# A decoder trunk on one core: the order of twelve-matmul blocks in TensorE's queue

## The chip, the cores and the metric

The kernel runs on one NeuronCore of a Trainium2 chip. The metric is the time of one execution on the device in microseconds, the median of several. The engines are named as the profile names them: PE (TensorE; PEld is its weight load), DVE (VectorE), ACT (ScalarE), POOL (GpSimd) and SP (the queue that issues DMAs).

## What is computed

One inference step of a one-layer hybrid decoder trunk, for 1024 prompt positions and 8 decode positions, together T = 1032 columns, with 1024 features, in float32. Cut to what matters:

```python
def mixer(xn):                                   # xn = rmsnorm(x)
    qkv, z, xbc, dt = split(xn @ w_in)           # 1024 -> 7184 columns
    for g, (window, dil) in enumerate(((128, 1), (512, 4), (2048, 16))):
        q, k = rope(qkv[g, 0]), rope(qkv[g, 1])  # 8 heads of 64
        o[g], lse[g] = dilated_window_attention(q, k, qkv[g, 2])
    attn = merge(o, softmax(lse over g))
    y = ssd(silu(conv4(xbc)), dt)                # 16 heads, chunks of 128
    ssm = rmsnorm((y + d_skip * xs) * silu(z))
    return concat(attn, ssm) @ w_out             # 1536 -> 1024
x = x + rmsnorm(mixer(rmsnorm(x)))
x = x + rmsnorm((silu(h @ w_gate) * (h @ w_up)) @ w_down)   # h = rmsnorm(x), hidden 2816
```

The decode positions take part in the same products, attend to key and value caches and step an SSD state; the caches are also copied to the outputs, shifted by one row.

## The kernel before

Activations lie transposed, features on the 128 partitions and the T columns along the free axis, in three chunks of CW = 344 columns. Each large operand is split into a high part and a remainder (`wh` and `wl` of a weight, `hs` and `ls` of an activation; `xh`, `xl`, `hh`, `hl` and so on in the profile), and a product is the sum of three: high by high, remainder of the weight by high, high by remainder of the activation. `unit` (line 160) computes one 128 x 344 block of a product into a PSUM tile that way: for each of n blocks of 128 input features three matmuls, all at line 168. n is 8 for the products out of 1024 features, so 24 matmuls; 6 or 4 in the last product of the SwiGLU (18 or 12 matmuls), and 4 in the attention half of the output projection (12). `gemm` (line 181) loads one 128-column weight block (`load_w`, line 136), and for each chunk runs a unit in one of two PSUM tiles (`psg`) and copies or adds the result out.

The stages, in order of time: the norm of the input and the first 12 column blocks of `w_in` (`xb`, convolution of SSD); then, `pattern` (line 682) for the three attention patterns: for each of 4 head pairs (`hp`) `do_v`, `do_qk` for q and `do_qk` for k (three gemms of three units, copied to a row tile `rw` at line 576, of which there are two buffers), and `attend` (line 620). Beside the first pattern run the 16 calls of `ssd` (line 467), beside the others the decode scores. Then the 8 gemms for z, beside them the merge of the three patterns (written to `ah` and `al`, lines 848 and 849) and the decode attention over the cached values (line 869); then the output projection with its norm, and the SwiGLU in groups of hidden blocks, `pg` and `pu` for gate and up and `g` for the last product.

Work that is not a unit is called side work here. On PE it is many small matmuls and transposes: for `ssd`, `xt` (line 487), `gb` (493, 494), `yp` (513), `yo` (521) and `stp` (529); for attention, `sps` (636, scores of two tiles of 128 queries for each of two heads of 64 features), `ptp` (657, transposes of the exponentials), `nps` (670, by the values, 64 output rows per head), and `vtp` (594, transposes of the values, copied to `vt` at line 596). A tile of 128 queries (`j`, eight per head pair) goes sps, maximum (DVE, 642), exponential (ACT, 650), `ptp`, copy (661 or 663), `nps`. PSUM holds two `sps` tiles and one each for `ptp` and `nps`; q, k and v of two head pairs fit in SBUF. Rope of q and k is side work on ACT, POOL and DVE, and ends at line 610 with `qr`.

The order on every engine is laid out when the program is built. Each instruction carries a number, `tc.cur_priority`, and the framework walks along a timeline of its own model (`schedule_with_timeline_sim=True`): at each step an engine takes, of the instructions whose inputs and buffers are ready there, the one with the lowest number. On the chip each engine then runs its list in that fixed order and waits where an input is not there yet. The numbers come from counters that `prio` (line 54) takes up and puts back, so that within one kind the order is that of the program:

```python
ctr = {"evac": 1_000_000, "w": 5_000_000, "side": 10_000_000, "late": 20_000_000, "main": 50_000_000}
```

"evac" are the copies out of PSUM and the statistics of the norms (matmuls at lines 215, 921 and 990), "w" the loads and splits of weights, "side" the side work, "late" the merge and decode attention, and "main" the matmuls of `unit`, of line 361 (the dt columns) and of line 945 (the first units of the output projection, written out). So a unit's matmuls fill PE wherever no side instruction is ready.

Of the kernel before, what the change touches and what calls it, by code (L numbers as in the profile page):

```python
# [16 lines left out]
P = 128  # L17
# [19 lines left out]
RATE = (0.35, 0.52)  # L37
NEG = -1e30
SCALE = 0.125

PC_NORM = 0
PC_CW = PC_NORM + 5 * 8
# [5 lines left out]

def trunk(tc, a, o):
    nc = tc.nc  # L50
    ctr = {"evac": 1_000_000, "w": 5_000_000, "side": 10_000_000, "late": 20_000_000, "main": 50_000_000}

    @contextmanager
    def prio(kind):
        old, tc.cur_priority = tc.cur_priority, ctr[kind]
        yield
        ctr[kind], tc.cur_priority = tc.cur_priority, old
# [35 lines left out]
    for g in range(NG):  # L93
        w = WIN[g]
        n = (w - 1) * 1024
# [64 lines left out]
    def unit(ps, w, hs, ls, c, ch=CH):  # L160
        wh, wl = w
        c0, c1 = ch[c]
        n = len(hs)
        with prio("main"):
            for k in range(n):
                ws = slice(k * P, (k + 1) * P)
                for j, (x, y) in enumerate(((wh, hs[k]), (wl, hs[k]), (wh, ls[k]))):
                    nc.tensor.matmul(ps, x[:, ws], y[:, c0:c1], start=(k == 0 and j == 0),  # L168
                                     stop=(k == n - 1 and j == 2))

    gpools = [psg]
    ngp = [0]
# [1 line left out]
    def gps(name="g", cw=CW):  # L174
        q = gpools[ngp[0] % len(gpools)]
        ngp[0] += 1
        if q is psg:
            return q.tile([P, 512], F32, tag="g", name=name)[:, :cw]
        return q.tile([P, 512], F32, tag="ap", name=name)[:, :cw]

    def gemm(src, cols, hs, ls, evac, cc=(0, 1, 2), share=False):
        w = load_w(src, cols, share)
        for c in cc:
            ps = gps()
            unit(ps, w, hs, ls, c)
            with prio("evac"):
                next_copy(evac(c, ps))
# [110 lines left out]
    for m in range(12):  # L298
# [8 lines left out]
        if m == 0:  # L307
            gpools.extend((psg, psa, psa, pst, psn))
            begun = {}
            for c in range(3):  # L310
                for q in range(2):
                    begun[q, c] = gps()
                    unit(begun[q, c], first[q], xh, xl, c)
# [43 lines left out]
    for c, (c0, c1) in enumerate(CH):  # L357
        ps = gps("dps")
# [261 lines left out]
    def attend(g, hp, qr, kr, vt):  # L620
        nh = nhp.tile([P, S], F32, tag="nh", name="nh")
        for j in range(8):
# [16 lines left out]
            for h in range(2):  # L639
# [5 lines left out]
            i2 = slice(hp * 2, hp * 2 + 2)  # L645
            nc.vector.tensor_scalar(out=ngm[:, g, j, i2], in0=mx[:, g, j, i2], scalar1=-SCALE, scalar2=0.0,  # L646
                                    op0=ALU.mult, op1=ALU.add)
            for h in range(2):
                i = hp * 2 + h
                nc.scalar.activation(out=sm[:, h, :nk], in_=sm[:, h, :nk], func=AF.Exp, scale=SCALE,  # L650
                                     bias=ngm[:, g, j, i:i + 1], accum_out=den[:, g, j, i:i + 1])
# [105 lines left out]
    with prio("side"):  # L757
# [3 lines left out]
        for h in range(2):  # L761
            nc.vector.tensor_reduce(out=dmx[:, h:h + 1], in_=sal[:, h].rearrange("p g x -> p (g x)"), op=ALU.max,
                                    axis=AX.X)
        nc.vector.tensor_scalar(out=dmx, in0=dmx, scalar1=-SCALE, scalar2=0.0, op0=ALU.mult, op1=ALU.add)
        for h in range(2):
            sv = sal[:, h].rearrange("p g x -> p (g x)")
            nc.scalar.activation(out=sv, in_=sv, func=AF.Exp, scale=SCALE, bias=dmx[:, h:h + 1],
                                 accum_out=dde[:, h:h + 1])
# [5 lines left out]
        for g in range(NG):  # L774
# [3 lines left out]
                             start=True, stop=True)  # L778
# [26 lines left out]
    with prio("late"):  # L805
# [11 lines left out]
        for g in range(NG):  # L817
            t = cap.tile([P, 8, 8], F32, name=f"wg{g}")
            nc.vector.tensor_tensor(out=t, in0=sn[g][:, :, 0:8], in1=mm, op=ALU.subtract)
            nc.scalar.activation(out=t, in_=t, func=AF.Exp, scale=SCALE)  # L820
            wg.append(t)
# [113 lines left out]
    def ssm_w(m, share=False):  # L935
        return load_w(a["w_out"][m][:, 512:1536], 1024, share)

    ws = [ssm_w(m) for m in range(2)]
    pq = [[gps() for c in range(2)] for m in range(2)]
    with prio("main"):  # L940
        for k in range(KT):
            for m in range(2):
                for j in range(3):
                    for c in range(2):
                        nc.tensor.matmul(pq[m][c], ws[m][j == 1][:, k * P:(k + 1) * P],
                                         (sl if j == 2 else sh)[k][:, CH[c][0]:CH[c][1]],
                                         start=(k == 0 and j == 0), stop=(k == KT - 1 and j == 2))
# [45 lines left out]
    for c, (c0, c1) in enumerate(CH):  # L993
# [4 lines left out]
        for m in range(KT):  # L998

            def ev(c, ps, m=m, acc=acc):  # L1000
                r = nc.vector.tensor_tensor(out=mix[m][:, c0:c1], in0=mix[m][:, c0:c1], in1=ps, op=ALU.add)
                stat(mix[m][:, c0:c1], m == 0, acc, nc.vector)
                return r

            if m % 2 == 0:
                pair = kept[m] if m in kept else load_pair(m, False)
            ps = gps()
            unit(ps, [x[:, (m % 2) * 512:(m % 2 + 1) * 512] for x in pair], ahs, als, c)
            with prio("evac"):
                ev(c, ps)  # L1010
        with prio("evac"):
# [3 lines left out]
            for m in range(KT):  # L1015
                if m % 2 == 0:
                    x = np_.tile([P, 2, CW], F32, tag="xr", name="xr")
# [247 lines left out]
```

## Time and profile before

| | |
|---|---|
| median of 3 runs | 1928.76 us (1927.81 to 1932.84) |
| the profiled execution | 1929.59 us |
| its span, first to last instruction | 1927.8 us |
| instructions on PE | 11727 matmul records, 95% of the span busy |
| DVE, ACT, POOL busy | 53%, 38%, 20% |
| mean granted clock of PE | 0.979 |

The profile is of one execution. The busy time of PE is the union of its matmuls' records; consecutive matmuls overlap in it (a record of 0.32 us every 0.16 us), so a start-to-start distance tells more than a duration. A small float32 matmul or transpose stands as two records. "Idle before" is time in which the engine stood still before an instruction, with what released it. The granted clock is PE's clock as a share of 2.4 GHz.

### The profile page before, as it was taken

The page shows a single profiled execution, that of the slowest core. Times are in us where ns is not written, and L with a number is a line of the kernel's source. Part 1 is how long each engine was busy: PE and PEld are TensorE (multiplying, and loading weights), DVE is VectorE, ACT ScalarE, POOL GpSimd, SP SyncE. Part 2 cuts the span into 40 slices and gives each one's busy share as a digit, 9 for nine tenths or more (in the row PEclk, how much of TensorE's full clock was granted, in tenths as well). Part 3 has the DMA queues.
Part 4 walks back from the last instruction along what each step waited for, and adds up shares of the span by engine and source line. Part 5 has one row for each costly group of instructions (what it writes and reads, how often), then busy time and mean ns, then how long its engine had stood idle before and what let it go on. Part 6 is the DMA issues. An engine that isn't in the chain of part 4 may idle for free. (4 is left out here: it accounts for less than half of the span.)

```text
span 1927.8 us, 29260 instructions
## 1 busy us (share of the span) xinstructions
PE 1825.0 (95%) x11727; PEld 1709.3 (89%) x11727; DVE 1014.0 (53%) x1896; ACT 739.2 (38%) x1388; POOL 394.5 (20%) x277
## 2 busy tenths in 40 slices
PE   8999989999999899998879989999999999999994
PEld 6999878888888798887679989999999999999993
DVE  6544676757764544455774896331333333333348
ACT  5543554545554455665242353222221112211242
POOL 0000244543232311133533342000000000000025
PEclk9999999999999999999889999999999999999997
DMA  4322333443334433464754454347433643366362
GB/s 162 122 95 86 119 108 112 137 128 107 104 115 136 156 100 110 142 237 137 178 154 133 147 168 132 109 150 249 133 115 130 240 164 131 105 202 207 115 247 88
DMA packets 125544, 275.26 MB, mean 143 GB/s; under 512 B 17616, under 2 KB 83632, under 8 KB 124000
## 3 DMA queue, kind: packets, MB, share of 16 engines
q1 hardware_dynamic: 125408, 273.39, 43.4%
q8 instruction: 92, 1.51, 0.3%
q14 instruction: 44, 0.36, 0.1%
HBM read 235.86 MB, written 125.47 MB: 187 GB/s over the span
## 5 line engine op out<-in xcount | busy, mean ns | idle before, releaser
L168 PE MATMUL g<-xh,wh 128*128 128x344 f32 x1344 | 443.7, 330 | 9.7 <-ACT zt L893 5.5
L168 PE MATMUL g<-xl,wh 128*128 128x344 f32 x1344 | 440.4, 328 | 1.5 <-DVE xl L222 1.5
L168 PE MATMUL g<-xh,wl 128*128 128x344 f32 x1344 | 439.0, 327 | 0.5 <-DVE wl L157 0.5
L168 PEld LDWEIGHTS g<-xh,wh 128*128 128x128 f32 x1344 | 255.8, 190 | 19.3 <-ACT zt L893 6.1
L168 PEld LDWEIGHTS g<-xh,wl 128*128 128x128 f32 x1344 | 256.2, 191 | 11.3 <-issue 9.9
L168 PEld LDWEIGHTS g<-xl,wh 128*128 128x128 f32 x1344 | 256.3, 191 | 10.4 <-issue 7.4
L157 DVE TENSOR_TENSOR wl<-wr,wh 128x1024 fp32r<-128x1024 f32 (+1 forms) x133 | 163.0, 1226 | 124.9 <-ACT wh L156 124.7
L156 ACT CAST wh<-wr 128x1024 fp32r<-128x1024 f32 (+1 forms) x133 | 134.4, 1011 | 214.5 <-PE g L168 128.8
L168 PE MATMUL pg<-fh,wl 128*128 128x344 f32 x504 | 161.8, 321 | 0.2 <-DVE wl L157 0.2
L168 PE MATMUL pg<-fl,wh 128*128 128x344 f32 x504 | 161.8, 321 | 0.0
L168 PE MATMUL pu<-fl,wh 128*128 128x344 f32 x504 | 161.6, 321 | 0.0
L168 PE MATMUL pu<-fh,wh 128*128 128x344 f32 x504 | 161.2, 320 | 0.0
L168 PE MATMUL pu<-fh,wl 128*128 128x344 f32 x504 | 160.8, 319 | 0.0
L168 PE MATMUL pg<-fh,wh 128*128 128x344 f32 x504 | 158.5, 322 | 0.0
L1110 POOL TENSOR_TENSOR ow<-wr,ow 128x512 fp32r<-128x512 f32 x8 | 11.1, 1407 | 674.9 <-ACT ow L1109 674.9
L168 PE MATMUL g<-hl,wh 128*128 128x344 f32 x432 | 138.0, 319 | 0.0
L168 PE MATMUL g<-hh,wl 128*128 128x344 f32 x432 | 137.6, 319 | 0.0
L168 PE MATMUL g<-hh,wh 128*128 128x344 f32 x432 | 137.3, 320 | 0.0
L230 DVE TENSOR_TENSOR u<-pu,rf 128x344 f32<-128x344 f32 x66 | 34.1, 516 | 195.5 <-PE pu L168 195.5
L650 ACT ACTIVATE sm<-sm,ngm 128x128 f32<-128x128 f32 (+1 forms) x192 | 84.9, 443 | 108.3 <-DVE ngm L646 106.2
L606 POOL TENSOR_TENSOR sw<-sw,sin 128x1032 f32<-128x1032 f32 x24 | 74.9, 3122 | 247.6 <-ACT sw L605 184.1
L1079 ACT CAST hh<-s 128x344 fp32r<-128x344 f32 x66 | 31.7, 480 | 199.4 <-DVE s L1078 197.3
(323 smaller groups left out, 3710.7 us busy)
## 6 DMA issues: line engine op xcount, KB each, us to landing
out_skv<-in_cache SPq DMA_DIRECT2D x64, 1023.5 KB, 5.3
wr<-in_w_in SPq DMA_DIRECT2D x56, 512.0 KB, 3.8
wr<-in_w_fin SPq DMA_DIRECT2D x44, 512.0 KB, 3.8
out_skv<-in_cache SPq DMA_DIRECT2D x16, 1022.0 KB, 5.5
wr<-in_w_out SPq DMA_DIRECT2D x24, 512.0 KB, 4.1
wr<-in_w_fout SPq DMA_DIRECT2D x24, 384.0 KB, 4.2
e<-cs_d SPq DMA_DIRECT2D x16, 512.0 KB, 3.9
n_d<-nh SPq DMA_DIRECT2D x12, 512.0 KB, 4.2
```

What stands on the lines that cost most here:

```text
L156: nc.scalar.copy(wh[:, :cols], wr[:, :cols])
L157: nc.vector.tensor_tensor(out=wl[:, :cols], in0=wr[:, :cols], in1=wh[:, :cols], op=ALU.subtract)
L168: nc.tensor.matmul(ps, x[:, ws], y[:, c0:c1], start=(k == 0 and j == 0), stop=(k == n - 1 and j == 2))
L230: return nc.vector.tensor_tensor(out=dst, in0=ps, in1=r[:dst.shape[0], c0:c1], op=ALU.mult)
L606: nc.gpsimd.tensor_tensor(out=sw[:, 0:T], in0=sw[:, 0:T], in1=sin, op=ALU.mult)
L650: nc.scalar.activation(out=sm[:, h, :nk], in_=sm[:, h, :nk], func=AF.Exp, scale=SCALE, bias=ngm[:, g, j, i:i + 1], accum_out=den[:, g, j, ...
L1079: nc.scalar.copy(hh[:, c0:c1], s)
L1110: nc.gpsimd.tensor_tensor(out=wl, in0=src, in1=wh, op=ALU.subtract)
```

## The change

The twelve consecutive matmuls of a unit that begin at a multiple of twelve are kept together: the first keeps the number kind "main", the other eleven get the new kind "run", whose numbers lie behind "evac" and ahead of "w", "side" and "late". A unit of 24 is two such blocks, one of 12 is one, one of 18 a block of twelve and one of six. `unit` also returns its last matmul, which nothing uses. Lines 361 and 945 are as before.

```diff
@@ -37,6 +37,7 @@
 SCALE = 0.125
+RUN = 12
@@ -48,7 +49,7 @@
-    ctr = {"evac": 1_000_000, "w": 5_000_000, "side": 10_000_000, "late": 20_000_000, "main": 50_000_000}
+    ctr = {"evac": 1_000_000, "run": 3_000_000, "w": 5_000_000, "side": 10_000_000, "late": 20_000_000, "main": 50_000_000}
@@ -161,12 +162,14 @@
         n = len(hs)
-        with prio("main"):
-            for k in range(n):
-                ws = slice(k * P, (k + 1) * P)
-                for j, (x, y) in enumerate(((wh, hs[k]), (wl, hs[k]), (wh, ls[k]))):
-                    nc.tensor.matmul(ps, x[:, ws], y[:, c0:c1], start=(k == 0 and j == 0),
-                                     stop=(k == n - 1 and j == 2))
+        for k in range(n):
+            ws = slice(k * P, (k + 1) * P)
+            for j, (x, y) in enumerate(((wh, hs[k]), (wl, hs[k]), (wh, ls[k]))):
+
+                with prio("main" if (3 * k + j) % RUN == 0 else "run"):
+                    last = nc.tensor.matmul(ps, x[:, ws], y[:, c0:c1], start=(k == 0 and j == 0),
+                                            stop=(k == n - 1 and j == 2))
+        return last
```

## Rows read from the trace of the kernel before

**Rows 1.** The page, part 1: busy time, share and instructions of each engine.

```profile
PE 1825.0 (95%) x11727; PEld 1709.3 (89%) x11727; DVE 1014.0 (53%) x1896; ACT 739.2 (38%) x1388; POOL 394.5 (20%) x277
```

**Rows 2.** By stage: length, PE PEld DVE ACT POOL busy, granted clock, DMA, GB/s.

```profile
200.00:600.00 400.00, 383.21 (x2701) 329.18 (x2699) 269.06 (x629) 208.69 (x426) 162.86 (x112) 0.99 0.40 122
600.00:975.00 375.00, 346.60 (x2233) 304.42 (x2234) 199.92 (x455) 188.95 (x400) 107.54 (x58) 0.96 0.47 147
...
1177.00:1890.00 713.00, 709.85 (x4489) 709.38 (x4488) 251.11 (x399) 155.25 (x254) 21.17 (x16) 1.00 0.47 160
```

**Rows 3.** The same view for line 168 alone, the stage of side work.

```profile
200.90:970.90 770.00, 532.50 (x3003) 479.05 (x3002) 0.98 0.43 135
```

**Rows 4.** The chain that ended last, 1190 to 1205 us: start, us, what.

```profile
1193.35 3.78 PE pg L168 x24
```

**Rows 5.** Timeline of PE around two bursts: start, us, instruction [idle before].

```profile
453.18 0.32 PE L168 MATMUL g<-xh,wl 128*128 128x344 f32 x1
453.44 0.66 PE L670 MATMUL nps<-pt,vt 128*64 128x128 f32 x8
...
455.07 0.32 PE L168 MATMUL g<-xl,wh 128*128 128x344 f32 x1
455.22 0.60 PE L487 MATMUL xt<-ident,xg 128*128 128x128 f32 x4
...
456.01 0.41 PE L168 MATMUL g<-xh,wh 128*128 128x344 f32 x1
456.25 0.32 PE L168 MATMUL g<-xh,wl 128*128 128x344 f32 x1
```

**Rows 6.** Timeline of PE: the first and the last of 190 bursts.

```profile
200.95 0.66 PE L427 MATMUL dtp<-ident,dex 8*128 8x8 f32 x8
...
969.99 0.85 PE L921 MATMUL ptp<-acc,ones 128*128 128x344 f32 x2 [2.45 <-POOL acc L908]
```

**Rows 7.** Waits of PE, 200 to 975 us: total us, times, longest us.

```profile
PE sps L636 <- DVE qr L610: 9.9, 5, 3.8
PE xt L487 <- DMA xg<-xs_d: 7.4, 4, 2.3
PE nps L869 <- DVE cvt L868: 6.3, 3, 3.2
...
PE nps L670 <- DVE pt L663: 3.7, 3, 1.7
...
```

**Rows 8.** Windows (columns of rows 2), then timeline of PE at three places.

```profile
444.00:450.00 6.00, 6.00 (x59) 4.26 (x58) 4.42 (x4) 1.71 (x6) 5.18 (x2) 1.00 0.24 92
...
599.80:606.60 6.80, 5.13 (x20) 4.48 (x21) 5.66 (x14) 0.00 (x0) 3.28 (x2) 0.50 0.59 195
...
601.47 0.80 PE L636 MATMUL sps<-qr 64*128 64x128 f32 x4 [3.79 <-DVE qr L610]
...
444.11 0.66 PE L670 MATMUL nps<-pt,vt 128*64 128x128 f32 x8
...
449.84 0.42 PE L168 MATMUL g<-xh,wl 128*128 128x344 f32 x1
```

**Rows 9.** `ptp` by line, 756 to 800 us, and timeline of PE between two.

```profile
L657 PE MATMUL ptp<-ident,sm x16: 272/273/332, 760.3 to 791.8; 128*128 128x128 f32 x16
...
764.56 0.44 PE L657 MATMUL ptp<-ident,sm 128*128 128x128 f32 x2
...
769.18 0.44 PE L657 MATMUL ptp<-ident,sm 128*128 128x128 f32 x2
```

**Rows 10.** Timeline of ACT, second head pair.

```profile
287.89 0.61 ACT L596 COPY vt<-vtp 128x512 f32<-128x512 f32 x1
...
301.73 0.43 ACT L576 COPY rw<-g 128x344 f32<-128x344 f32 x1
```

**Rows 11.** Timeline of DVE and of PE where the merged attention is used.

```profile
1035.43 0.43 DVE L849 TENSOR_TENSOR al<-nt,ah 128x256 fp32r<-128x256 f32 x1
...
1049.88 0.32 PE L168 MATMUL g<-ah,wah 128*128 128x344 f32 x1
```

## The prediction

> **What bounds the kernel now.** I read the page first: TensorE (PE) is busy for 95% of the span, the next engine for 53% [rows 1]. So the time is PE's work plus the places where PE waits or works slowly. The table by stage says where those are [rows 2]: from 1177 us to 1890 us, the SwiGLU, PE shows no gap (709.85 of 713 us), and a unit of 24 long matmuls (line 168) takes 3.78 us there [rows 4], so one costs 0.157 us in a dense row. Nothing but long products stands in that stage, so keeping twelve together changes nothing in it, nor in most of the first 163 us. The change can act between about 200 and 970 us, where attention, SSD and decode (side work) share PE with 3003 long matmuls [rows 3].
>
> In that stage the timeline of PE shows 190 bursts of side instructions between long matmuls, the first at 200.95 us and the last at 969.99 us [rows 6]. Counted there, 74 of the 189 rows of long matmuls between two bursts have at most 12 of them, 88 have 13 to 24, and 27 have more. Three losses hang on the bursts:
> - A change-over. After a burst of transposes the next two long matmuls start 0.24 us apart (456.01 and 456.25) in place of 0.157: 0.08 lost. Eight `nps` matmuls start 0.26 us after the long one ahead of them (453.18 and 453.44): 0.10 lost on the way in [rows 5].
> - Waits in PE's fixed order: PE reaches a side instruction before its input is there. `sps` 9.9 us, `xt` 7.4, `nps` of decode 6.3, `nps` of attention 3.7: 27.3 us in 15 waits, the longest 3.8 [rows 7].
> - The clock. Granted 0.99 over 400 us and 0.96 over 375 us [rows 2] are together some 38 us at the lower of the two levels (1.2 GHz). In 599.8 to 606.6 us it is 0.50 all through, and PE stood still for 3.79 us of that, waiting for `qr`, up to 601.47 us [rows 8]: the clock falls where PE stands still.
>
> **The change part by part.** No instruction, DMA or wait is added or taken out, and SP, POOL, ACT and DVE keep their rules; only PE's order moves. The first of each twelve keeps the number of "main", behind all side work; the other eleven get 3 million, ahead of "w", "side" and "late" and behind "evac". So the 3003 long matmuls become 250 blocks of 12 x 0.157 = 1.88 us, and a side instruction that becomes ready inside a block waits for its end, 0.94 us on average. The statistics of the norms (L215, L921, L990) go at "evac" and still break in; the products at L361 and L945 are written apart and keep "main".
>
> *Fewer bursts.* Bursts that become ready in one block join. If 190 fall on 250 block ends at random, 250 x (1 - e^(-190/250)) = 133 ends carry one: 57 fewer at most. Steps of one chain can't join, since the second needs the first, so the other end is none fewer. I take 45, nearer the upper end because attention, SSD and decode are three chains side by side. A joined burst saves one way out and, for tiled operands, one way in: 0.08 to 0.20 us, say 0.15 [rows 5]. Gain 45 x 0.15 = 7 us; ends 0 and 11.
> The rows show that a burst that begins with 64-wide operands (`nps`) costs 0.10 us on entry, and one that begins with full 128 x 128 transposes starts 0.15 us after the last long matmul, so nothing [rows 5]. The Trainium skill, TensorEngine Tiling, section Key Properties, says that changing the tiling mode drains TensorE, which this agrees with. By that rule joined bursts still pay for each change between tiled and full operands inside them, so only the way out would be saved: 45 x 0.09 = 4 us in place of 7.
>
> *Waits in PE's order.* A side instruction that is placed up to 1.88 us later finds its input more often ready. A wait of x under 1.88 us shrinks on average to x^2/3.76, a longer one by 0.94 us. Their mean is 27.3 / 15 = 1.8 us (the four of `xt` come to 7.4 us with 2.3 the longest), so about half is left: 27 to some 14, gain 13 us. Ends: 0 (every input moves back as far as its reader) and 27.
>
> *The clock.* The 38 us at 1.2 GHz cost at most half of themselves, 19 us [rows 2], less where PE stands still anyway, as in 5.13 busy of 6.80 us [rows 8]. Where waits shrink, some of these stretches go: I take a quarter, 5 us; ends 0 and 10.
>
> *What gets later.* Each PE step of a side chain now waits for a block. Attention is the longest chain: transpose a tile's scores (`ptp`), copy, multiply (`nps`), next tile. In the last pattern eight `ptp` bursts (16 records) stand between 760.3 and 791.8 us, 4.5 us apart [rows 9], with 22 long matmuls between the two at 764.56 and 769.18 us [rows 9]. Rounded up to two blocks that is 24, 0.3 us more per tile and 2.4 us per head pair, 29 us over the 12 pairs. If the input is ready just after the second block ends, it is 36: long products then run ahead of attention, and as they may not run far, PE is left with nothing to do in about one tile of four for some 3 us (4.5 less the burst itself and a chain without waits). That is 8 x 0.25 x 3 = 6 us per pair, 72 over the 12.
> What hides a lag: the transposes read by the `vt` copy at 287.89 us free a row buffer, and the product that needs it is first copied at 301.73 [rows 10], 13 us later; two products wait in PSUM beside it, 2 x 3.77 us. So about 21 us of lag are free; beyond it PE waits, `rw` copies first. At the end the last `al` is written at 1035.43 us and first read at 1049.88 [rows 11]: another 14 us at least. So the cost lies between 0 (29 less 21 and 14) and 72 - 21 = 51 us. I take 10, near the lower end, since the 22 in the rows lies under 24.
>
> **Sum.** -7 - 13 - 5 + 10 = -15 us. The profiled execution took 1929.6 us (span 1927.8 and 1.8 around it), 0.8 above the median of the runs, so the forecast is 1928.8 - 15, **1914 us**.
>
> **Rivals.** What a measurement can tell from no change is about 0.3%, 5.8 us.
> - *The waits move with their inputs.* The order is laid out on a modelled timeline; delayed steps delay their successors in it too, so PE still arrives early, and the 7 us of change-overs are taken back by the lag. For it: `qr` waits come from DVE's own queue, which stays 67% busy in 200 to 600 us [rows 2]. Against: block ends only ever push a reader later. Time: 1929 - 7 + 7 = about 1928. Chance 0.20; that the blocks hardly form (second matmuls whose `wl` is late) ends here too.
> - *Attention becomes the bound.* Place: `ptp` and `nps` of lines 657 and 670. It decides once a tile needs a third block: if its input comes over 1.9 us after the block end that served the tile before, plus the burst. At half of all tiles it costs 36 - 21 = 15 us, at all tiles 51; less 7 for change-overs, 1937 to 1973. I put it at the nearer half, about 1942: in the SSD stretch DVE is shared by three chains, and there rows of long matmuls over 24 are not rare (27 of 189). Against: 22 and 23 are the commonest spacings in the last pattern. Chance 0.20.
> - *Longer bursts lower the clock.* A joined burst leaves PE for several us on transposes and small float32 products. The longest without a wait, from 444.11 to 449.84 us, has a granted clock of 1.00 from end to end [rows 8]. The Trainium skill, TensorE: Matmul & The Clock Gate, Part 4, says that a transpose doesn't count as PE activity in the same way; by that rule such bursts would drop the clock, which the trace doesn't show so far. If 15 joined bursts each brought 3.4 us (half the stretch in [rows 8]) at half speed, that would be 15 x 1.7 = 26 us more, less 7: 1948. Chance 0.06.
> - *All waits go.* -11 - 27 - 10 with no lag: about 1881. Chance 0.04.
>
> **Numbers.** The forecast has 0.50. Its own range: net gains of 6 (below that it is "same") to 34 (the 25 of gains and 9 more of their upper ends, no lag) give 1895 to 1923. Faster takes it and the last rival, 0.54; same 0.20; slower 0.20 + 0.06 = 0.26. For eight in ten the range leaves out the full waits at the low end and the all-tiles end of attention: 1893 to 1946.
>
> **What would show it.** Right: the same 3003 long matmuls in rows of 12 and 24; bursts down from 190 to about 145; waits of PE on `sps`, `xt` and decode `nps` down to about half; fewer stretches at 0.50; 1177 to 1890 us unchanged in length. `ptp` bursts of the last pattern 4.5 to 4.8 us apart. Wrong: spacings of 36 and new PE waits on `rw` or `zt`, which is attention as the bound; a clock under 1 after bursts without a wait; or the side stage as long as before with the same waits on other lines.

## The result: slower by 1.0%

The changed kernel takes 1948.68 us (median of 4 runs, 1945.8 to 1949.82) against 1928.28 us of the kernel before on the same chip (4 runs, 1926.64 to 1932.84): a ratio of 1.0100, 95% interval 1.0079 to 1.0121. The forecast was 1914 us, with a range of 1893 to 1946; so the sign was wrong, and the time lies 2.7 us above the range. The profiled execution took 1945.8 us, its span 1944.0 us (1927.8 before).

The page of the changed kernel, part 1 (answers to [rows 1]), then the table by stage (columns as in [rows 2]). Lines of the kernel from `unit` on are moved down by 2 or 3: 168 is now 170, 576 is 579, 898 is 901.

```profile
PE 1828.3 (94%) x11727; PEld 1715.1 (88%) x11727; DVE 1028.1 (53%) x1896; ACT 742.8 (38%) x1392; POOL 395.0 (20%) x277
```

```profile
200.00:600.00 400.00, 377.52 (x2672) 328.62 (x2671) 274.08 (x628) 205.07 (x422) 154.54 (x106) 0.98 0.36 110
600.00:975.00 375.00, 346.48 (x2227) 304.83 (x2226) 189.21 (x431) 190.29 (x396) 102.01 (x58) 0.94 0.47 148
829.00:975.00 146.00, 127.28 (x751) 108.38 (x750) 80.80 (x171) 75.81 (x144) 53.78 (x34) 0.89 0.53 161
975.00:1195.00 220.00, 192.04 (x1108) 182.41 (x1107) 177.54 (x222) 88.36 (x144) 94.21 (x58) 0.94 0.52 158
1196.00:1909.00 713.00, 710.07 (x4505) 709.58 (x4504) 252.00 (x403) 156.22 (x257) 21.19 (x16) 1.00 0.47 161
```

The SwiGLU is what it was, 710.07 of 713 us [rows 2]. What is lost is lost ahead of it: the last norm statistic of the mixer is at 1194.54 us (L993), before at 1175.23 us (L990). These 19.3 us, less 3 us by which the rest is shorter, are the 16.2 us of span.

The waits of PE from 200 to 975 us (total, times, longest) show what took the place of [rows 7]:

```profile
PE g L170 <- ACT rw L579: 22.3, 12, 7.3
PE nps L872 <- DVE cvt L871: 5.8, 3, 4.1
PE sps L639 <- DVE mx L645: 4.7, 4, 2.4
PE nps L673 <- ACT pt L664: 4.7, 1, 4.7
PE sps L639 <- DVE qr L613: 2.7, 1, 2.7
...
PE nps L673 <- DVE pt L666: 1.5, 4, 0.6
```

The waits of side work for its inputs are down: `qr` from 9.9 to 2.7 us, `xt` from 7.4 to nothing. A wait of another kind has come: PE stands at the first matmul of a unit until ACT has copied an earlier unit into a row buffer, 22.3 us. In the longest of them everything that held the buffer can be read (timeline of all engines around 260 us):

```profile
253.16 2.83 DVE L461 TENSOR_TENSOR hs<-hs,tm 128x512 f32<-128x512 f32 x1 [4.37 <-POOL tm L457]
255.91 1.22 DVE L610 TENSOR_TENSOR rw<-rw,cos 128x1032 f32<-128x1032 f32 x1
257.24 2.10 DVE L613 TENSOR_TENSOR qr<-rw,sw 128x1024 f32<-128x1024 f32 x1
259.26 0.15 DVE L614 TENSOR_TENSOR dec<-rw,sw 128x8 f32<-128x8 f32 x1
259.52 0.79 ACT L579 COPY rw<-g 128x344 f32<-128x344 f32 x2 [6.99 <-DVE dec L614]
260.02 0.66 PE L170 MATMUL g<-xh,wh 128*128 128x344 f32 x1 [7.32 <-ACT rw L579]
```

The rope of an earlier product (L610 to L614) stands behind a step of the decode state on DVE; till it is through, both row buffers are full, and PE has run out of long matmuls that may start.

**The balance up to 829 us.** In both kernels the last of 108 row copies comes at nearly the same time (828.5 us before, 829.1 after). From start to start of PE's records between 200 and 829 us, less the idle time, long matmuls take 416.8 us before (2436 of them) and 408.4 after (2422), side work 188.4 and 188.1, idle time 23.6 and 32.3. The three fill the same 629 us in both, so what tells is the work done in them. Long matmuls take 8.4 us less, but 14 fewer stand in the stretch; at 0.169 us in place of 0.171 for one, the blocks saved about 6 us. PE stood idle 8.7 us longer, and some side work was still to come: from 829 to 975 us it takes 31.2 us in place of 21.7.

**Behind 829 us** the loss appears. Attention has fallen behind: the last copy of a head pair's result (`nh`) ends at 298.98 us in place of 282.30 in the first pair, 932.7 in place of 894.1 in the last. And the loads of `y`, which the z stage multiplies with, are issued late. The last transposes of values and the loads before (timelines of PE and SP); then the same after, with more of PE's and ACT's; last SP's wait for the first load (waits of SP, 800 to 1000 us: total, times, longest). The x4 of `vtp` are four transposes: a transpose stands as one record, a small matmul as two, so the "eight `nps` matmuls" of the prediction are four.

```profile
844.86 0.60 PE L594 MATMUL vtp<-ident,vp 128*128 128x128 f32 x4
...
847.62 0.34 SPq L898 DMA_DIRECT2D yg<-y_d  x1
850.19 1.37 SPq L898 DMA_DIRECT2D yg<-y_d  x3
852.86 3.26 SPq L898 DMA_DIRECT2D yg<-y_d  x4
```

```profile
861.30 0.42 ACT L896 COPY zt<-g 128x344 f32<-128x344 f32 x1
...
872.26 0.69 PE L673 MATMUL nps<-pt,vt 128*64 128x128 f32 x4 [4.67 <-ACT pt L664]
...
882.18 1.11 PE L597 MATMUL vtp<-ident,vp 128*128 128x128 f32 x4
...
883.33 3.95 SPq L901 DMA_DIRECT2D yg<-y_d  x8
...
889.31 0.77 ACT L896 COPY zt<-g 128x344 f32<-128x344 f32 x2
```

```profile
SPq L901 <- PE vtp L597: 1.9, 1, 1.9
```

The buffers of `yg` lie in memory that the row pools held. The last reader there is the last transpose of the values (`vtp` of `vp`, L597): it starts at 882.18 us, takes 1.11 (0.60 before, at the higher clock), and the loads follow at 883.33. It is late because it shares the one PSUM tile of `ptp` and so stands behind the attention of the pair before. While `y` is missing, no z buffer comes free: no row of z leaves PSUM between 861.30 and 889.31 us, and PE has only small steps of attention and decode. Its clock falls to the lower level for 23.9 us. The same stretch before, then two stretches after (columns of [rows 2]):

```profile
862.00:890.00 28.00, 26.71 (x184) 23.55 (x183) 19.15 (x45) 17.82 (x39) 7.45 (x5) 0.99 0.43 137
```

```profile
862.00:890.00 28.00, 18.30 (x101) 13.32 (x100) 16.04 (x51) 13.54 (x33) 7.58 (x6) 0.66 0.55 193
...
871.20:895.10 23.90, 17.92 (x82) 13.60 (x83) 10.94 (x45) 10.99 (x37) 4.92 (x3) 0.50 0.61 231
```

The last z copy comes at 985.16 us (975.61 before), 9.6 us late. Another 9.8 us is lost up to the last norm statistic, where the output projection has to wait until the merged attention is written: ACT's copy of a weight's high part (`wah`) stands until the last `al` (answers to [rows 11]; timeline of DVE, ACT and PE):

```profile
1063.66 0.42 DVE L852 TENSOR_TENSOR al<-nt,ah 128x256 fp32r<-128x256 f32 x1
1064.12 2.00 ACT L972 CAST wah<-wr 128x1024 fp32r<-128x1024 f32 x2 [0.49 <-DVE al L852]
1065.26 1.84 PE L170 MATMUL g<-ah,wah 128*128 128x344 f32 x4 [8.10 <-ACT wah L972]
```

The slack of 14 us there before is used up: `al` is 28 us later, and PE waits 8.10 us.

### The profile page after: what moved, and what is told of

Read it like the earlier page. It is cut to its first block, busy times and chain, and to the rows that moved or that the text cites. A ratio compares the mean times of both kernels' runs of the same rounds, so it can differ in the third digit from the quotient of the medians.

```text
span 1944.0 us, 29271 instructions
## 1 busy us (share of the span) xinstructions
PE 1828.3 (94%) x11727; PEld 1715.1 (88%) x11727; DVE 1028.1 (53%) x1896; ACT 742.8 (38%) x1392; POOL 395.0 (20%) x277
## 5 line engine op out<-in xcount | busy, mean ns | idle before, releaser
L170 PE MATMUL g<-xh,wh 128*128 128x344 f32 x1344 | 451.1, 336 | 24.5 <-ACT rw L579 22.3
L170 PE MATMUL g<-xl,wh 128*128 128x344 f32 x1344 | 435.0, 324 | 1.5 <-DVE xl L225 1.5
L170 PE MATMUL g<-xh,wl 128*128 128x344 f32 x1344 | 434.0, 323 | 0.5 <-DVE wl L158 0.5
L608 ACT COPY sw<-rw 32x1032 f32<-32x1032 f32 x96 | 101.0, 1052 | 2.6 <-DVE dec L614 1.2
```

The source lines that it names most:

```text
L170: last = nc.tensor.matmul(ps, x[:, ws], y[:, c0:c1], start=(k == 0 and j == 0), stop=(k == n - 1 and j == 2))
L608: nc.scalar.copy(sw[q * 32:(q + 1) * 32, 0:T], rw[s * 32:(s + 1) * 32, :])
```

## The experiments

Each is timed in five rounds against the kernel before on the same chip; times are medians, brackets hold the 95% interval of the ratio. "Gate" stands for the time at which the loads of `y` start. For most of them blocks are switched on and off while the kernel is built, with 1 in place of RUN where they are off (then every matmul is "main", as before):

```diff
+    run = [RUN]
-                with prio("main" if (3 * k + j) % RUN == 0 else "run"):
+                with prio("main" if (3 * k + j) % run[0] == 0 else "run"):
```

**Run 1, blocks up to the end of the second pattern** (`run[0] = 1` before `pattern(2)`).

> Blocks of twelve up to the second attention pattern, single matmuls in TensorE's order from the third pattern on. Theory A (the loss sits in the third pattern: attention lags there behind the long products, its last value transposes come 34 us later, and the loads of y for the z products wait for the SBUF they free): the first sps of the 7th head pair comes at about 595 us as in the changed kernel, the y loads at about 845 us as before, and the time is 1918 to 1928 us. Rival B (the loss sits in the first two patterns, where the long products wait 20 us for the copies of rw): the time stays at 1938 us or more. Rival C (a lower clock after longer bursts): fewer than half of the lost 20 us come back, 1938 us or more, with stretches at half clock that follow no wait.

1929.6 us, 1.0014 [1.0004 to 1.0024]. Far from the 1938 of the rival; above the 1918 to 1928 of the theory by 2. The lag is there all the same (`nh` of the first pair at 299.8 us), but the gate opens at 866 us, and the last z copy is not late (970.5 us, 975.6 before). The gain that the theory expected is not there either.

**Run 2, blocks in the third pattern alone.**

> The reverse: single matmuls everywhere but in the products of the third pattern, which are in blocks of twelve. Theory A: attention of the third pattern loses some 25 to 35 us against the long products, y loads at 870 us or later, time 1940 to 1950 us. Rival B: about the time of before, 1923 to 1934 us.

1932.6 us, 1.0027 [1.0015 to 1.0038]: the 1940 to 1950 missed. The lag builds up anew (23 us at the eleventh pair, 11 at the last), and the gate opens at 865 us. Neither part makes the whole loss by itself.

**Run 3, the change with the last value transposes in another PSUM tile.** The transposes of the third pattern's values no longer stand behind attention; nothing else is edited.

```diff
-                tp = att_ps("vtp")
+                tp = side_ps("vtp") if g == 2 else att_ps("vtp")
```

> The changed kernel, with the value transposes of the third pattern in the PSUM tiles that the SSD used (idle by then) in place of the tile that they share with ptp; so they need not queue behind the attention of the pair before, and the row of values is free early. Nothing else is changed. Theory A: the y loads come 20 to 35 us earlier than in the changed kernel, the gap in the z products at 861 to 889 us closes, and most of the loss goes: 1925 to 1937 us (the end of attention stays late, so the 8 us wait for the merged attention may stay). If the lag of attention costs by another way than the y loads: 1943 us or more.

1927.33 us, 1.0003 [0.9991 to 1.0015]: the loss is gone, as a sum. Loads of `y` from 852.37 us, and in the stretch that was at half clock PE is full (windows of this run, then timeline of PE):

```profile
871.20:895.10 23.90, 23.90 (x169) 21.07 (x169) 15.29 (x44) 17.39 (x35) 6.67 (x4) 1.00 0.40 144
...
1051.25 0.63 PE L170 MATMUL g<-ah,wah 128*128 128x344 f32 x1 [4.02 <-issue]
```

The move does more than open the gate. Attention no longer shares its PSUM tile in the third pattern: the tenth pair ends at 813.5 us (824.9 with the change). The last z copy comes at 974.26 us in place of 985.16, and of the wait at `wah` 4.02 us are left of 8.10. No run moves the loads of `y` alone, so what the gate costs by itself is read from the trace.

**Run 4, the same move in the kernel before**, its control.

> The same move of the value transposes, in the kernel before. It is the control for the run above: before, the y loads came at 847 us and the z products had no such gap, so theory A expects little, 1922 to 1932 us. If it gains as much as the run above, that run shows nothing about blocks.

1923.47 us, 0.9982 [0.9973 to 0.9992]. Without blocks the move is worth 3.5 us (0.0018), with them 18.7 (0.0097). So most of it is not a gain that stands beside the change; it takes away what the change did. With the move the blocks still lose 0.0021, 4 us.

**Run 5, blocks through all three patterns, off from z on** (`run[0] = 1` behind `pattern(2)`), and **run 6, blocks from z on only.**

> Blocks of twelve in everything up to the last product of the third attention pattern, single matmuls from the z products on. Blocks only up to the second pattern cost 2 us and only in the third pattern 5 us, the change costs 20. Theory A1 (what is left comes from blocks beside the z products, where the last two head pairs still run): about the sum of the two, 1932 to 1938 us, y loads near 865 us. Theory A2 (the lags of the early and the third pattern add up and reach a point where the z products stop): 1942 to 1950 us, y loads at 875 us or later.

> Blocks of twelve only from the z products on, single matmuls before. Theory A1 (blocks beside the z products cost most): 1936 to 1945 us. Theory A2 (only a lag that was built up before counts): 1925 to 1932 us, the y loads near 850 us.

Run 5: 1939.91 us, 1.007 [1.0057 to 1.0083], between the two ranges and nearer to the lags that add up: gate at 879 us, where runs 1 and 2 had 866 and 865. Run 6: 1926.28 us, 0.9987 [0.9976 to 0.9998], as the lags that add up have it. So most of the loss is made ahead of z and paid there; the 0.0030 between run 5 and the change are about as wide as their intervals.

**Run 7, attention's matmuls of the third pattern ahead of the blocks** (a kind "att": 2_000_000 for `sps`, `ptp` and `nps`, so that they may go in inside a block; one of the three places is shown).

```diff
+                    with (prio("att") if g == 2 else ExitStack()):
                         nc.tensor.transpose(tp[:, q * P:(q + 1) * P], sm[:, h, b * P:(b + 1) * P], ident)
```

> The changed kernel, but in the third pattern the matmuls and transposes of attention (sps, ptp, nps) may break into a block; decode, SSD and merge still wait for its end. Theory A (attention's wait for block ends is what it loses by): y loads at 855 us or earlier, 1924 to 1934 us. If it is the waits of other side work, or the blocks by themselves: 1942 us or more.

1941.43 us, 1.0076 [1.0058 to 1.0094]: theory A missed, and just short of the other range. The lag comes into the third pattern ready made, and the gate is still at 883 us.

**Run 8, blocks of six** (`RUN = 6`).

> Blocks of six in place of twelve. Theory A: a side step waits half as long, and as the last value transposes have slack before the z products need their SBUF, less than half of the loss stays: 1926 to 1937 us, y loads between 850 and 870 us. If the number of change-overs counted: between the kernels, nearer the changed one, 1938 us or more.

1944.67 us, 1.0088 [1.0071 to 1.0106]: theory A missed. The time lies in the range given for change-overs, but the trace shows the gate again. The first pair is late by 11 in place of 17 us, but the eleventh ends at 872 us (841 before), and the gate opens at 875. Half the length does not halve the cost.

**Run 9, attention's matmuls ahead of the blocks in all three patterns**, and **run 10, that with the move of run 3.**

> The change, with the PE instructions of attention (scores, transposes of the exponentials, product by the values) of all three patterns numbered ahead of the blocks, so that they may go in inside a block. Theory A: the lag of attention, which is there from the first head pair on (its end 299.0 us with the change, 282.3 without), is made by attention's own PE steps waiting for the ends of blocks. Then the first pair ends by 290 us, the loads of y are issued by 866 us (881.4 with the change, 847.6 without), and the time is 1923 to 1934 us. Rival B: the lag comes from the other side work (SSD, transposes of the values) waiting for blocks and holding DVE and ACT in their order. Then the first pair ends at 295 us or later, the loads of y come after 875 us, and the time is 1937 us or more.

> The kernel of the run before with the transposes of the values of the third pattern in the other PSUM tile as well. If A holds and the gate of the y loads is all that is left of the loss: loads of y by 850 us, and 1919 to 1927 us. If blocks cost something behind the gate too (the merge of attention late): 1928 to 1934 us.

Run 9: 1956.6 us, 1.0154 [1.0131 to 1.0176], slower than the change. The place of the lag is as the theory has it, the time is not. `nh` of the first pair in run 9 (ACT's timeline), then SSD's last step `stp` (line view of PE: count, min/median/max, first and last start) and PE's waits from 200 to 600 us:

```profile
279.12 0.59 ACT L682 COPY nh<-nps 128x512 f32<-128x512 f32 x1 [3.03 <-PE nps L676]
```

```profile
L532 PE MATMUL stp<-xdd,bt x32: 590/591/697, 220.7 to 649.3; 128*128 128x512 f32 x32
```

```profile
PE sps L640 <- DVE qr L613: 11.8, 3, 8.7
PE g L170 <- ACT rw L579: 10.1, 5, 5.5
```

Attention is on time again in the first pattern (279.7 us, before 282.3, in the first pair, 463.8 and 466.9 in the fourth), as theory A has it. But the new number also puts attention's steps ahead of all of SSD's on PE, which the kernel before does not do, so the run does not show whether the lag comes from waiting for blocks or for SSD. SSD now waits in its place: its last step starts at 649.3 us, before at 572.5, with the change at 597.9. The products are done 17 us later than before (845.6 us), and the gate opens at 873 us (with the change at 883.33, not at the 881.4 of the expectation). Run 10: 1932.41 us, 1.0039 [1.0023 to 1.0054], in the range given for a cost behind the gate; its products too are late (843.8 us).

**Run 11, blocks from z on with the moved transposes.**

> Blocks only from the products of z on, and the transposes of the values of the third pattern in the other PSUM tile. If the gains of the two single changes (1923.47 against 1927.9, and 1926.28 against 1928.4) add: 1920 to 1923 us. If both are the same gain, the end of the z products coming earlier: 1923 to 1927 us.

1928.93 us, 1.0006 [0.9996 to 1.0016]: both ranges missed. The gains of runs 4 and 6 do not add here. The trace shows a place and no cause: the last z copy comes at 971.14 us, 1.9 us ahead of run 4, and then PE stands still until ACT has copied a weight's high part, a wait that run 4 does not have (timeline of PE):

```profile
1017.67 0.94 PE L171 MATMUL g<-sh,wh 128*128 128x344 f32 x2 [5.86 <-ACT wh L158]
```

**Runs 12 and 13, the value transposes of all patterns moved, in the change and in the kernel before** (`tp = side_ps("vtp")`).

> The change, with the transposes of the values of all three patterns in the other PSUM tile (run 3 moved those of the third pattern alone). Theory A: the long products, brought forward by the blocks, stand still on row buffers that hold values whose transposes wait behind the attention of the pair before. Then PE's waits on the row copies from 200 to 600 us (21.6 us with the change) fall below 10, the last row copy comes by 820 us (829.1), and the time is 1910 to 1922 us. Rival B: the row buffers are held by the rope of q and k on POOL and DVE, which queue behind SSD work; then those waits stay at 18 us or more and the time is that of run 3, 1924 to 1931 us.

> The kernel before with the same move in all three patterns; the control of the run beside it, and the step after the version of run 4 (1923.47 us). A: values no longer hold a row buffer in any pattern, a few us less than run 4: 1916 to 1922 us. B: nothing more to gain, since products go behind all side work anyway: 1922 to 1927 us.

2100.98 us, 1.0889 [1.0869 to 1.091], and 2117.72 us, 1.0987 [1.0965 to 1.1008]: neither theory, and no test of what they were meant for. In the first pattern those tiles belong to SSD, which comes first in the program, so already the first pair's value transposes stood behind all of SSD: in run 13 the first starts at 506.22 us, SSD's last step at 504.31. ACT's timeline in run 13, and its windows:

```profile
243.00 0.42 ACT L576 COPY rw<-g 128x344 f32<-128x344 f32 x1
...
507.96 0.79 ACT L576 COPY rw<-g 128x344 f32<-128x344 f32 x2 [0.43 <-PE vtp L594]
```

```profile
300.00:400.00 100.00, 29.13 (x132) 20.44 (x132) 37.89 (x77) 10.20 (x16) 41.16 (x38) 0.53 0.34 101
```

The products stop dead from 243 to 508 us: a row buffer that is held stops every long matmul behind it. That is the change's `rw` wait at its extreme. The two runs differ in the blocks alone, and here the blocks gain 16.7 us (2117.72 less 2100.98), where all pairs but the first run without SSD beside them. That gave the next question.

**Run 14, blocks from the third pattern on, and run 15, from the second on, both with the move of run 3.**

> Blocks from the third pattern on (after SSD), with the transposes of the values of the third pattern in the other PSUM tile. Runs 12 and 13 differ in the blocks alone, and there the blocks gain 17 us, 9 of them on the eleven head pairs that run without SSD beside them. Theory A: blocks gain where SSD is not beside attention; the third pattern is four of those pairs and z comes behind: 1916 to 1922 us, below run 4 (1923.47). Rival B: the lag of attention in the third pattern (decode scores share DVE there, run 2) takes it back: 1924 to 1931 us.

> The same with blocks from the second pattern on, whose first half still has SSD beside it. Theory A: the second half gains, the first loses: 1917 to 1926 us. Rival B: the lag adds up from the second pattern on and reaches the merge, as in run 3 (1927.33): 1926 to 1932 us.

Run 14: 1921.35 us, 0.9962 [0.9947 to 0.9977]. Run 15: **1916.79 us, 0.9945 [0.9932 to 0.9957]**, faster than both kernels and than run 4. In run 15 the loads of `y` start at 835.88 us and the last z copy at 958.87 (973.08 in run 4):

```profile
835.88 1.21 SPq L903 DMA_DIRECT2D yg<-y_d  x2
...
958.87 0.42 ACT L898 COPY zt<-g 128x344 f32<-128x344 f32 x1
```

**Run 16, run 15 without the move, and run 17, blocks only up to the end of the first pattern.**

> Blocks from the second pattern on; the transposes of the values as in the change (not moved). Theory A: the loss of the change is made in the first pattern, where SSD is beside every head pair; without blocks there the lag reaches the tenth pair at about 851 us in place of 881, the loads of y are issued by 866 us, and the time is 1917 to 1928 us. Rival B: any lag at the value transposes opens the gate late, and run 15 was good by the move alone: loads of y after 870 us and 1932 us or more.

> Blocks up to the end of the first pattern only; nothing moved. Theory A: this part alone brings the loss of products' time and starts the lag of 17 us: 1930 to 1940 us, loads of y 860 us or later. Rival B: the lag made there is worked off in two patterns without blocks: 1925 to 1930 us, loads of y by 855 us.

Run 16: 1944.78 us, 1.0094 [1.0077 to 1.0111], its rival: without blocks in the first pattern the gate still opens at 881 us. Run 17: 1938.55 us, 1.0057 [1.0043 to 1.0070], as the theory has it: products done at 839.2 us, SSD's last step at 598.8, loads from 859 (860 or later was expected). PE's waits in run 17, 200 to 600 us, and the loads of `y` in run 16:

```profile
PE g L171 <- ACT rw L580: 20.7, 7, 7.6
```

```profile
880.94 3.80 SPq L903 DMA_DIRECT2D yg<-y_d  x8
```

The ratios together:

| blocks | value transposes as they were | last ones moved |
|---|---|---|
| none | 1 | 0.9982 |
| everywhere (the change) | 1.0100 | 1.0003 |
| from the second pattern on | 1.0094 | 0.9945 |
| from the third pattern on | not run | 0.9962 |
| from z on | 0.9987 | 1.0006 |
| up to the end of the first pattern | 1.0057 | not run |
| up to the end of the second pattern | 1.0014 | not run |
| up to the end of the third pattern | 1.0070 | not run |
| in the third pattern alone | 1.0027 | not run |

Read across, the move takes 0.0097, or 19 us, from the change, and 0.0149, 29 us, from blocks from the second pattern on; without blocks 3.5 us. Read down in the right column, blocks from the second pattern on gain 0.0037 (7 us), and blocks up to the end of the first lose 0.0058 (11 us); run 17 finds the same 11 us without the move. So, along this path, the change's 19 to 20 us are: 7 gained, 11 lost up to the end of the first pattern, 15 (19 less the 3.5 that the kernel before pays too) at the shared tile and the gate. Each step has the runs' uncertainty of some 2 to 4 us.

The parts do not simply add. In the left column blocks in the first pattern cost 11 us alone, but only 0.0006 when they come on top of blocks from the second on, where the gate is late already; and blocks in the second pattern on top of the first gain 0.0043. Nor is the gate's cost in proportion to its lateness: at 865 and 866 us (runs 1 and 2) the last z copy comes at 970.5 and 976.3, about as before; at 875 to 883 (runs 8, 5, 16 and the change) it comes at 983 to 989. A late gate is not all, either: in run 17 it opens at 859, and the last z copy comes at 986.9, since the products ahead of z are late.

## Why the prediction was wrong

**Fewer bursts: right.** 190 bursts became 137 from 200 to 975 us (145 forecast), with 12, 24 or 36 long matmuls between them (50, 65 and 19 times; twice 60). The saving of about 6 us on long matmuls up to 829 us stands against a forecast of 7 for the whole stage. By the rule of the Trainium skill (TensorEngine Tiling, section Key Properties), with only the way out saved, the 50 bursts that went there would be worth 50 x 0.09 = 4.5 us, and at the prediction's 0.15 us 7.5. The trace's 6 lie between the two, and 10 us more of that stretch are at the lower clock, so it does not decide.

**Waits in PE's order: the total was right, and worth nothing.** The four inputs of 27.3 us [rows 7] cost 14.7 now (`qr` 2.7, `xt` 0, decode `nps` 5.8, attention's `nps` 4.7 and 1.5), against a forecast of 14. In its parts that is luck: `xt` went altogether, decode's `nps` hardly moved, and `sps` on `mx` adds 4.7 that were not there. But 22.3 us of waits on `rw` came (3.1 before from 200 to 600 us, 21.6 after), which the text had as a sign of error. The term of 13 us took a shorter wait for a gain; PE's idle time up to 829 us rose by 8.7 us. PE's time was free only as long as there was a long product allowed to start; two row buffers, emptied by rope and value transposes, set how many there are. The blocks let products run ahead early (the third pair's last row copy 14 us earlier, 324.7 in place of 338.4 us), and PE then stood idle for what it had won.

**The clock: wrong sign.** From 200 to 975 us PE is at the lower level for 59 us (34 before); forecast was a quarter less. Each of the 12 stretches from 200 to 1200 us holds a standstill of PE or comes just behind one, as in [rows 8]: 7.32 us at 260.02, 4.67 at 872.26, and in the weakest case 1.36 up to 924.39. Not each standstill brings one: 2.48 us up to 448.87 does not. The rival that bursts of transposes lower it by themselves, by the rule of TensorE: Matmul & The Clock Gate, Part 4 in the Trainium skill, is not borne out: the change's trace has no such stretch without a standstill. It is a weak test, since its bursts are not of transposes alone.

**The lag: the step that failed.** The term of +10 us rests on lag being hidden. "So about 21 us of lag are free", then "another 14 us at least": the cost of what gets later was taken as 10 us. The size of the lag was met (29 us forecast over 12 pairs; 39 are there at the last), but by luck: it was to grow by 2.4 us per pair, and 17 us are there after the first. What it may not do was looked for in two places, the row buffers and the use of `al`. Each of them was real (the `rw` waits; the 8.10 us at `wah`), but a third was not looked for: the loads of `y`, not on any chain of the trace of before, go into a buffer that takes over the memory of the row pools, freed by the last value transposes. No view of before shows it as a wait, since it opened in time (the last `vtp` at 844.86 us, the first load at 847.62); it had to be found by asking of each late step which memory it holds. In place of the 10 us, the late value transposes cost the change 19 us (run 3 against it), 15 more than they cost the kernel before (run 4).

**"Attention becomes the bound"** (0.20, about 1942 us) is nearest in its signs, spacings of 36 and waits on `rw`. Nearest in time is the rival of the clock, 1948 us, by luck, since its mechanism is not in the trace. That attention's `ptp` steps wait for a third block is not what happened in the last pattern: only one of the 19 spacings of 36 lies from 730 to 829 us, ten lie up to 487 us. The step from tile to tile in the ninth pair is about 4.9 us (four `nps` between 741.71 and 756.45 us), just over the 4.5 to 4.8 forecast. The lag came in the first pair, at one go, and again in the third pattern; and where attention went ahead of every block (run 9), SSD was late in its place.

**What stays open**: why attention of the first pair falls 17 us behind; how the 11 us of the first pattern divide among row buffers, a late SSD and the clock; what the gate costs apart from the rest of the lag; and run 11.

## What to carry to other kernels

A saving on a busy engine is worth something only where that engine has work that may start; when filler work is moved forward, look first at the buffers it fills. Before an off-path chain is allowed to lag, list every buffer and every reuse of memory that its last step releases, and the transfers that wait for them: a trace shows no wait for a release that comes just in time. If a reordering loses, try it stage by stage: here the same blocks lose 11 us up to the end of the first pattern and gain 7 from the second on, once the value transposes are out of the way.

## What was not expected of the hardware

With PE starved to small steps of attention and decode, the clock stayed at 0.50 for 23.9 us on end (871.2 to 895.1 us), though PE was busy for 17.92 of them, and it rose when long products came back. In run 13 it was 0.53 over 100 us with 29.13 busy. So a starved stretch is paid twice: the long products wait, and the small steps that they wait for are slower too (four `vtp` take 1.11 us there, 0.60 at the higher clock). The number of such stretches from 200 to 1200 us hardly rose (11 before, 12 after), but their sum went from 55 to 85 us.
